# Attention's written order on TensorE: two scores ahead of each group's first transposes, and the first scores of a half spread out

## The chip, the cores and the metric

The kernel runs on one core of a Trainium2 chip. A core has five engines with a queue of instructions each: TensorE (PE, matrix products and transposes), VectorE (DVE), ScalarE (ACT), GpSimd (POOL) and SyncE (SP, which here issues transfers only). The metric is the time of one execution on the device in microseconds (us): the median of three runs of the kernel before is 2747.23 us (2744.07 to 2749.85).

## What is computed

One step of a one-layer encoder with two parallel mixers, on a prompt of 2048 rows and a sample of 64 rows with 4096 cached positions, width 1024. A combined projection gives q, k, v, gates and the input of a pooling branch. The attention branch has 8 heads of 128 and is "stick-breaking": no softmax, but a running product over the keys.

```python
    z = jnp.einsum('bqhd,bkhd->bhqk', q, k,
                   preferred_element_type=jnp.float32) * (SB_HEAD_DIM ** -0.5)
    mask = kpos[None, :] < qpos[:, None]
    log_beta = jax.nn.log_sigmoid(z)
    log_1m = jnp.where(mask, log_beta - z, 0.0)
    after = lax.cumsum(log_1m, axis=3, reverse=True) - log_1m
    a = jnp.where(mask, jnp.exp(log_beta + after), 0.0)
    out = jnp.einsum('bhqk,bkhd->bqhd', a, v.astype(jnp.float32))
```

So the weight of a key is sigmoid(z) times the product of 1 - sigmoid(z) over all later keys. The rest of the layer (pooling, gates, two output products, a merge, a residual and a norm) is not touched here.

## The kernel before

Every product is made in three matmuls, high by high, high by low and low by high part, from operands split by `split` (L77): a copy to the narrow form on ScalarE (L82) and a subtraction on VectorE or GpSimd (L83).

The prompt is done in two halves of 1024 rows. In a half, `heads_phase` (L842) goes over the heads: while head `hd + 1` is projected (`head_proj`, L482, through `proj`, L291), the attention of head `hd` runs between. `run` (L118) does the interleaving: each of its generators yields a step with its estimated length in ns, and `run` always takes the one that has had the smallest share of its total so far. A projection step is six matmuls. The estimates are written by hand: `mm_ns` (L107) for a matmul, `head_ns` (L619) for the attention of a head, `slab_ns` (L310) for the projections. `run` also adds the lengths to `clock`, by which deferred work (`defer`, L110, such as writing k and v out through transposes on PE, `natural`, L468) is started.

The attention of a half is a `Stream` (L605). Its units are tuples (head, block of 512 queries, chunk of 512 keys, i), newest chunk first, and four units with i = 0 to 3 make a group: one block of queries against one chunk of keys. A group whose chunk is the block itself is diagonal and is only partly computed. In the first half a head has 12 units, in the second 28. Three steps belong to a unit:

- `scores(n)`: three matmuls of 128 queries against the chunk (L641 to L643) into a bank `z`. Then `weights_of_block` (L580): two sigmoids on ScalarE (L585 `om`, L586 `be`), in diagonal groups two masks on GpSimd (L577), the carry of the chunk before copied by GpSimd (L590), a scan along the keys on VectorE (L595), the carry out (L597, GpSimd) and a multiply on VectorE (L598) that leaves the weights in `be`.
- `transposes(n)`: for 128 keys of the chunk, the weights of all the group's four query rows (in a diagonal group those from i on) are turned on PE (L654) and split into `a`, high and low. So the first `transposes` of a group needs `be` of all its four scores.
- `products(n)`: three matmuls of the values with `a` (L669 to L671); the third uses the low part.

`steps` (L680) sets the order: with n counting up, it yields `scores(n)`, `transposes(n - 4)`, `products(n - 5)`.

On PE the program's order is the order written (the whole kernel runs under a manual schedule for PE, L1519). In the heads' phases the order on the other engines is chosen by the scheduler of the framework, from readiness and program order. Tiles live in rings: eight `be`, three `om`, two `a`, and two banks each for `z`, `tr` and the projections' `pj`.

Of the kernel before, what the change touches and what calls it, by code (L numbers as in the profile page):

```python
# [15 lines left out]
P = 128  # L16
# [28 lines left out]
def kernel(  # L45
# [31 lines left out]
    def split(hi, lo, src, eng=None):  # L77

        if eng == "v":
            nc.vector.tensor_copy(hi, src)  # L80
        else:
            nc.scalar.copy(hi, src)  # L82
        (nc.gpsimd if eng == "g" else nc.vector).tensor_tensor(lo, src, hi.bitcast(F32), op=ALU.subtract)  # L83
# [23 lines left out]
    def mm_ns(n):  # L107
        return max(107.0, n * 0.4167)
# [37 lines left out]
    with ExitStack() as front:  # L146
# [433 lines left out]
        def weights_of_block(z, off, carry, diag=False, be=None):  # L580

            if be is None:
                be = attp.tile([P, 528], F32, name="be", tag="be", bufs=8)
            om = attp.tile([P, 513], F32, name="om", tag="om", bufs=3)
            nc.scalar.activation(om[:, off:512], z[:, off:512], AF.Sigmoid, scale=-SCALE)  # L585
            nc.scalar.activation(be[:, off:512], z[:, off:512], AF.Sigmoid, scale=SCALE)  # L586
            if carry is None:
                nc.gpsimd.memset(om[:, 512:513], 1.0)
            else:
                nc.gpsimd.tensor_copy(om[:, 512:513], carry)  # L590
            if diag:
                strictly_causal(om[:, 384:512], 1.0)
                strictly_causal(be[:, 384:512], 0.0)
            rev = om[:, off:513][:, ::-1]
            nc.vector.tensor_tensor_scan(rev, rev, rev, 1.0, op0=ALU.mult, op1=ALU.bypass)  # L595
            nxt = attp.tile([P, 1], F32, name="carry", tag="carry", bufs=10)
            nc.gpsimd.tensor_copy(nxt, om[:, off:off + 1])  # L597
            nc.vector.tensor_tensor(be[:, off:512], be[:, off:512], om[:, off + 1:513], op=ALU.mult)  # L598
            return be, nxt
# [5 lines left out]
        class Stream:  # L605
# [3 lines left out]
            def __init__(self, half):  # L609
                self.half = half  # L610
                self.units = [(hd, qb, c, i) for hd in range(H) for qb in (2 * half + 1, 2 * half)
                              for c in range(qb, -1, -1) for i in range(4)]
                self.n = 0
                self.be = {}
                self.carry = {}
                self.split = {}
                self.att = {}

            def head_ns(self, hd):  # L619
                return sum(3 * mm_ns(P * (i + 1)) + (4 - i) * 109 + 3 * mm_ns(P * (4 - i)) if c == qb else 1732.0  # L620
                           for h_, qb, c, i in self.units if h_ == hd)

            def scores(self, n):
                hd, qb, c, i = self.units[n]
                out = heads[self.half, hd]
                diag = c == qb
                for cc in range(2 * self.half - 1, -1, -1):
                    if cc in out["k"]:
                        continue
                    for kind, chunk in (("k", kchunk), ("v", vchunk)):  # L630
                        raw = attp.tile([P, 512], F32, name=f"{kind}back", tag=f"{kind}raw", bufs=2)
                        nc.sync.dma_start(raw, kvd[kind, hd, cc])
                        out[kind][cc] = chunk()
                        split(*out[kind][cc], raw, "g")
                khi, klo = out["k"][c]
                qhi, qlo = out["q"][qb]
                m = P * (i + 1) if diag else 512
                off = 512 - m
                z = psum.tile([P, 512], F32, name="z")
                qs = slice(i * P, (i + 1) * P)  # L640
                nc.tensor.matmul(z[:, off:512], qhi[:, qs], khi[:, 0:m], start=True, stop=False)  # L641
                nc.tensor.matmul(z[:, off:512], qhi[:, qs], klo[:, 0:m], start=False, stop=False)  # L642
                nc.tensor.matmul(z[:, off:512], qlo[:, qs], khi[:, 0:m], start=False, stop=True)  # L643
                be, self.carry[i] = weights_of_block(z, off, None if diag else self.carry[i], diag)
                self.be[hd, qb, c, i] = (be, off)
                return 3 * mm_ns(m)

            def transposes(self, n):
                hd, qb, c, j = self.units[n]
# [10 lines left out]
            def products(self, n):  # L660
# [16 lines left out]
                    nc.sync.dma_start(aT_d[hd * P:(hd + 1) * P, r0:r0 + 512], o)  # L677
                return 3 * mm_ns(512 - s.start)

            def steps(self, hd):  # L680

                end = len(self.units)
                while self.n < end + 5 and (hd is None or (self.n < end and self.units[self.n][0] == hd)):
                    n = self.n
                    self.n += 1
                    if n < end:
                        yield self.scores(n)
                    if 0 <= n - 4 < end:
                        yield self.transposes(n - 4)
                    if 0 <= n - 5 < end:  # L690
                        yield self.products(n - 5)


        def sample_stream():
# [135 lines left out]
            for n in range(-1, end + 2):  # L830
                if n + 1 < end:
                    yield from keys(n + 1)
                if 0 <= n < end:
                    yield scores(n)
                if 0 <= n - 1 < end:
                    yield transposes(n - 1)
                if 0 <= n - 2 < end:
                    yield products(n - 2)
# [338 lines left out]
    with tc.manual_schedule(engines={E.PE, E.DVE, E.Activation, E.SP}):  # L1177
# [4 lines left out]
        order = [(i, t, p) for i in range(2) for t in range(3) for p in range(7)]  # L1182
# [103 lines left out]
        for s, (i, t, p) in enumerate(order):  # L1286
            r = rf.pop(s)
            more = s - p + 7 < len(order)
            for cc in range(2):
# [5 lines left out]
                for j in range(2):  # L1295
                    c = 2 * cc + j
# [100 lines left out]
        for n, (_, r) in enumerate(pairs):  # L1397
            wo = {nm: wf.get((2, nm)) for nm in WFORMS}
            f = {nm: of.pop((n, nm)) for nm in ("a11", "a12", "s2", "s1")}
# [123 lines left out]
```

## Time and profile before

| What | Value |
|---|---|
| median of 3 runs | 2747.23 us |
| profiled execution, its own time | 2746.59 us |
| its span, first to last instruction | 2744.9 us |
| mean granted clock of PE | 0.994 |
| heads of the first half, about | 75 to 600 us |
| sample stream and the first half's gates, about | 600 to 1120 us |
| heads of the second half, about | 1160 to 1912 us |
| wait of the group's first transposes on `be`, as idle time | 3.4 us in 5 places |
| wait of the third product on the low part of `a`, as idle time | 3.4 us in 6 places |

A row of the timeline has a start in us from the start of the span, a length in us, the engine, the line, the operation, its tiles (out<-in) and shapes, and how many like it were merged. In brackets stands how long the engine had been idle before it, and what ended that. Matmuls overlap: a matmul's length includes its passage through the array, and the next starts before it ends. So idle time in brackets is shorter than the time that was lost, which is read from start to start.

### The profile page before, as it was taken

To read this page: it belongs to the slowest core of one execution; us is meant where nothing else is said; L and a number is where in the kernel's file an instruction comes from. 1 tells how busy PE (TensorE), PEld (TensorE's weight loads), DVE (VectorE), ACT (ScalarE), POOL (GpSimd) and SP (SyncE) were. 2 spreads that over 40 slices of the span, in tenths; PEclk is the share of its full clock that TensorE was granted. 3 is DMA by queue.
4 is the path that set the end of the run, shared out by engine and by line. 5 is a ranking of instruction groups with operands and counts; after the bars stand their busy time and mean duration, and the time that the engine had idled before them with its cause. 6 is when DMAs were issued, how large, how long until landed. Compare 5 with 4: busy or idle time off the path is not lost.

```text
span 2744.9 us, 41961 instructions
## 1 busy us (share of the span) xinstructions
PE 2700.3 (98%) x15136; PEld 2368.1 (86%) x15136; DVE 1831.3 (67%) x2866; ACT 1268.5 (46%) x2527; POOL 567.0 (21%) x1277
## 2 busy tenths in 40 slices
PE   8999999999999999999999999999999999999998
PEld 7988888888998989988888888888888889999886
DVE  5555555567777783487887888786454236777876
ACT  4445444455555553455555555564222223332443
POOL 1112222230000000222433333342004601111001
PEclk9999999999999999999999999999999999999999
DMA  4224222224444444312111211112236857786753
GB/s 133 87 89 128 73 73 73 77 94 153 151 155 152 148 146 145 100 35 66 48 38 54 58 47 50 54 43 85 94 104 215 270 179 269 258 289 223 250 162 119
DMA packets 343540, 342.32 MB, mean 125 GB/s; under 512 B 29969, under 2 KB 286465, under 8 KB 343330
## 3 DMA queue, kind: packets, MB, share of 16 engines
q1 hardware_dynamic: 328898, 292.69, 34.0%
q0 software_dynamic: 14432, 46.93, 4.8%
q8 instruction: 119, 1.95, 0.3%
q14 instruction: 91, 0.75, 0.1%
HBM read 230.90 MB, written 108.65 MB: 124 GB/s over the span
## 4 chain that ended last, share of the span: by engine, by line
PE 89%; DVE 5%; DMA 2%; issue 2%; ACT 1%; POOL 0%; SPq 0%; DVEq 0%; POOLq 0%; ACTq 0%
PE pj L299 17%; PE pj L300 17%; PE pj L301 17%; PE tr L654 4%; PE x L1083 3%; PE x L1085 3%; PE x L1087 3%; PE att L671 2%; PE att L670 2%; PE att L669 2%; PE z L643 2%; PE z L642 2%; PE z L641 2%; PE y L1083 2%; PE y L1085 2%; PE y L1087 2%
## 5 line engine op out<-in xcount | busy, mean ns | idle before, releaser
L299 PE MATMUL pj<-hhi,whi 128*128 128x512 f32 (+2 forms) x2568 | 929.7, 362 | 0.5 <-ACT hhi L886 0.5
L301 PE MATMUL pj<-hhi,wlo 128*128 128x512 f32 (+2 forms) x2568 | 902.7, 352 | 0.0
L300 PE MATMUL pj<-hlo,whi 128*128 128x512 f32 (+2 forms) x2568 | 901.9, 351 | 0.8 <-DVE hlo L889 0.7
L301 PEld LDWEIGHTS pj<-hhi,wlo 128*128 128x128 f32 x2568 | 487.3, 190 | 60.8
L299 PEld LDWEIGHTS pj<-hhi,whi 128*128 128x128 f32 x2568 | 489.5, 191 | 56.6 <-ACT hhi L886 1.2
L300 PEld LDWEIGHTS pj<-hlo,whi 128*128 128x128 f32 x2568 | 488.7, 190 | 56.0 <-DVE hlo L889 1.5
L595 DVE TENSOR_TENSOR_SCAN om<-om 128x513 f32<-128x513 f32 (+3 forms) x356 | 387.5, 1088 | 209.8 <-POOL om L577 108.1
L585 ACT ACTIVATE om<-z 128x512 f32<-128x512 f32 (+2 forms) x320 | 171.6, 536 | 320.1 <-PE z L643 270.5
L83 DVE TENSOR_TENSOR wlo<-raw,whi 128x512 fp32r<-128x512 f32 x244 | 174.4, 719 | 184.8 <-ACT whi L82 183.9
L597 POOL COPY carry<-om 128x1 f32<-128x1 f32 x356 | 78.6, 221 | 915.0 <-DVE om L595 871.5
L598 DVE TENSOR_TENSOR be<-be,om 128x512 f32<-128x512 f32 (+3 forms) x356 | 230.5, 647 | 33.3 <-ACT a L82 0.5
L82 ACT CAST whi<-raw 128x512 fp32r<-128x512 f32 x251 | 155.1, 623 | 173.3 <-PE pj L300 160.2
L82 ACT CAST a<-tr 128x512 fp32r<-128x512 f32 (+2 forms) x356 | 188.0, 528 | 100.2 <-PE tr L654 89.8
L83 DVE TENSOR_TENSOR a<-tr,a 128x512 fp32r<-128x512 f32 (+2 forms) x356 | 215.6, 606 | 25.0 <-ACT a L82 23.1
L654 PE MATMUL tr<-ident,be 128*128 128x128 f32 x1088 | 176.1, 274 | 6.0 <-DVE be L598 3.4
L654 PEld LDWEIGHTS tr<-ident,be 128*128 128x128 f32 x1088 | 136.2, 140 | 44.4 <-DVE be L598 8.5
L586 ACT ACTIVATE be<-z 128x512 f32<-128x512 f32 (+2 forms) x320 | 170.0, 531 | 0.0
L669 PE MATMUL att<-a,v 128*128 128x512 f32 (+1 forms) x320 | 132.6, 414 | 0.0
L577 POOL TENSOR_SCALAR_AFFINE_SELECT om<-om 128x128 f32<-128x128 f32 x128 | 50.6, 395 | 359.6 <-ACT om L585 345.9
L590 POOL COPY om<-carry 128x1 f32<-128x1 f32 x224 | 123.4, 551 | 2.7 <-DVE be L598 0.7
L671 PE MATMUL att<-a,v 128*128 128x512 f32 (+1 forms) x320 | 118.6, 371 | 3.7 <-DVE a L83 3.4
L643 PE MATMUL z<-khi,qlo 128*128 128x512 f32 (+2 forms) x320 | 116.8, 365 | 0.0
(333 smaller groups left out, 4758.1 us busy)
## 6 DMA issues: line engine op xcount, KB each, us to landing
raw<-in_w_in_dram SPq DMA_DIRECT2D x253, 256.0 KB, 3.0
sg<-sm_d SPq DMA_DIRECT2D x48, 352.0 KB, 6.5
kraw<-in_cache_k_dram SPq DMA_DIRECT2D x64, 256.0 KB, 3.2
vraw<-in_cache_v_dram SPq DMA_DIRECT2D x64, 256.0 KB, 2.9
sm_d<-sgm SPq DMA_DIRECT2D x48, 256.0 KB, 2.4
wraw<-tw_d SPq DMA_DIRECT2D x24, 512.0 KB, 4.2
out_dram<-nat SPq DMA_DIRECT2D x42, 256.0 KB, 3.3
r<-aT_d SPq DMA_DIRECT2D x12, 704.0 KB, 7.3
```

What stands on the lines that cost most here:

```text
L82: nc.scalar.copy(hi, src)
L83: (nc.gpsimd if eng == "g" else nc.vector).tensor_tensor(lo, src, hi.bitcast(F32), op=ALU.subtract)
L299: nc.tensor.matmul(ps[:, 0:n], whi[:, k], hhi[:, k, c0:c0 + n], start=k == 0, stop=False)
L300: nc.tensor.matmul(ps[:, 0:n], whi[:, k], hlo[:, k, c0:c0 + n], start=False, stop=False)
L301: nc.tensor.matmul(ps[:, 0:n], wlo[:, k], hhi[:, k, c0:c0 + n], start=False, stop=k == KT - 1)
L585: nc.scalar.activation(om[:, off:512], z[:, off:512], AF.Sigmoid, scale=-SCALE)
L595: nc.vector.tensor_tensor_scan(rev, rev, rev, 1.0, op0=ALU.mult, op1=ALU.bypass)
L598: nc.vector.tensor_tensor(be[:, off:512], be[:, off:512], om[:, off + 1:513], op=ALU.mult)
L643: nc.tensor.matmul(z[:, off:512], qlo[:, qs], khi[:, 0:m], start=False, stop=True)
L654: nc.tensor.transpose(tr[:, i * P:(i + 1) * P], be[:, off + j * P:off + (j + 1) * P], ident)
L669: nc.tensor.matmul(self.acc[:, s], vhi[:, js], ahi[:, s], start=first, stop=False)
L671: nc.tensor.matmul(self.acc[:, s], vhi[:, js], alo[:, s], start=False, stop=last)
```

## The change

`steps` no longer counts units but takes its steps from a list that the new `order` makes. For each group with first unit g it gives: scores g and g + 1, transposes g - 4, products g - 5; then scores g + 2, transposes g - 3, products g - 4; then scores g + 3, transposes g - 2, products g - 3; then transposes g - 1, products g - 2. Before, one score stood ahead of each transposes. The second part is `lead`: the first four scores of a half count 1500 ns more each in `run`, and so does their head in `head_ns`. The steps themselves are as they were.

```diff
-                self.att = {}
+                self.todo = list(self.order())
 
             def head_ns(self, hd):
-                return sum(3 * mm_ns(P * (i + 1)) + (4 - i) * 109 + 3 * mm_ns(P * (4 - i)) if c == qb else 1732.0
-                           for h_, qb, c, i in self.units if h_ == hd)
+                return sum((3 * mm_ns(P * (i + 1)) + (4 - i) * 109 + 3 * mm_ns(P * (4 - i)) if c == qb else 1732.0)
+                           + self.lead(n) for n, (h_, qb, c, i) in enumerate(self.units) if h_ == hd)
+
+            def lead(self, n):
+                return 1500.0 if n < 4 else 0.0
...
-                return 3 * mm_ns(m)
+                return 3 * mm_ns(m) + self.lead(n)
...
+            def order(self):
+                end = len(self.units)
+                for g in range(0, end + 4, 4):
+                    for i in range(4):
+                        for n in ((g, g + 1), (g + 2,), (g + 3,), ())[i]:
+                            if n < end:
+                                yield n, self.scores, n
+                        for f, n in ((self.transposes, g + i - 4), (self.products, g + i - 5)):
+                            if 0 <= n < end:
+                                yield g, f, n
+                yield end, self.products, end - 1
+
             def steps(self, hd):
 
-                end = len(self.units)
-                while self.n < end + 5 and (hd is None or (self.n < end and self.units[self.n][0] == hd)):
-                    n = self.n
-                    self.n += 1
-                    if n < end:
-                        yield self.scores(n)
-                    if 0 <= n - 4 < end:
-                        yield self.transposes(n - 4)
-                    if 0 <= n - 5 < end:
-                        yield self.products(n - 5)
+                while self.todo and (hd is None or (self.todo[0][0] < len(self.units)
+                                                    and self.units[self.todo[0][0]][0] == hd)):
+                    _, f, n = self.todo.pop(0)
+                    yield f(n)
```

## The prediction, made before the changed kernel was run

> **What bounds the kernel.** I read the busy table first, then the table by stretches, then the waits of TensorE (PE), then the timeline of single groups.
>
> ```profile
> PE 2700.3 (98%) x15136; PEld 2368.1 (86%) x15136; DVE 1831.3 (67%) x2866; ACT 1268.5 (46%) x2527; POOL 567.0 (21%) x1277
> PEclk9999999999999999999999999999999999999999
> 1160.00:1820.00 660.00, 653.98 (x3333) 538.18 (x3333) 537.69 (x733) 381.25 (x773) 227.16 (x550) 1.00 0.17 50
> PE tr L654 <- DVE be L598: 3.4, 5, 1.9
> PE att L671 <- DVE a L83: 3.4, 6, 0.6
> ```
>
> PE is busy in 98% of the span at full clock, in an order written out by hand. So an edit of that order can only take away, or add, moments in which PE stands still: nothing is computed more or less. The third row is the attention of the second half (columns: length, PE, weight loads, VectorE (DVE), ScalarE, GpSimd): PE is busy for 654.0 of 660 us and VectorE for 537.7, 81%. VectorE makes everything that attention waits for there. The two wait rows count only idle time behind modelled ends; I therefore take lost time from the starts in the timeline.
>
> Names: **S** is a unit's score step (three matmuls), **T** its transposes, **P** its three products, **J** a step of six projection matmuls. Four units, 0 to 3, make a group. T needs the weights `be` of all four scores of its group; P's third matmul (L671) needs the low part `a` that VectorE subtracts after its T.
>
> **What the change removes.** The wait of a group's first T for the fourth score's `be`. Before, one S stands between that score's own step and T; now there are two, and a T and a P more.
>
> ```profile
> 1358.70 0.83 PE L654 MATMUL tr<-ident,be 128*128 128x128 f32 x4
> 1359.29 0.48 PE L299 MATMUL pj<-hhi,whi 128*128 128x512 f32 x1
> 1428.46 0.60 PE L654 MATMUL tr<-ident,be 128*128 128x128 f32 x4
> 1428.82 0.48 PE L669 MATMUL att<-a,v 128*128 128x512 f32 x1
> 1429.13 0.40 PE L670 MATMUL att<-a,v 128*128 128x512 f32 x1
> 1430.09 0.50 PE L671 MATMUL att<-a,v 128*128 128x512 f32 x1 [0.56 <-DVE a L83]
> 1162.11 0.34 PE L643 MATMUL z<-khi,qlo 128*128 128x384 f32 x1
> 1162.67 0.50 PE L641 MATMUL z<-khi,qhi 128*128 128x512 f32 x1 [0.23 <-ACT be L586]
> 1165.56 0.85 PE L654 MATMUL tr<-ident,be 128*128 128x128 f32 x3
> 1168.36 0.33 PE L654 MATMUL tr<-ident,be 128*128 128x128 f32 x1 [1.94 <-DVE be L598]
> 1168.44 0.48 PE L299 MATMUL pj<-hhi,whi 128*128 128x512 f32 x1
> 1901.51 0.85 PE L654 MATMUL tr<-ident,be 128*128 128x128 f32 x4
> 1902.12 0.48 PE L299 MATMUL pj<-hhi,whi 128*128 128x512 f32 x1
> ```
>
> An undisturbed T of four takes 0.36 from its start to the next matmul (1428.46 to 1428.82). The one at 1358.70 takes 0.59, the last at 1901.51 takes 0.61, and the half's first at 1165.56 takes 2.88. From 578 to 1902 us there are 23 such places, together 7.0 us; the half's first is 2.5 of it. The 1500 ns of `lead` put J steps between the first four scores of a half; with them the fourth score's wait for a `z` bank goes too (1162.11 to 1162.67, 0.5 with its second matmul). The J steps that come early are missing later, so they cost nothing. I take all **7.5** as gone. The bound on the other side is that the half's start stays: 3.0 less.
>
> There are also waits of L671. At 1429.13 the third product starts 0.96 after the second where 0.23 is usual, so 0.73 is lost. This place comes six times (heads 1 to 6), 4.4 in all; in the new order one more J stands between that T and its P, 1.4 us, so I count it as gone (bound: it stays). Nine smaller ones add 1.8. Removed in all: 7.5 + 4.4 + 1.8 = **13.7**.
>
> **What it moves.** The last quarter of a group now has no score. T2 P1 T3 P2 follow the fourth score, and P2 comes one S earlier behind its T2 than before. I stepped through the picking rule of `run` with its own estimates (43,868 of attention against 40,963 of projection per head in the second half). For head 2, units counted in the half, the order was J S78 T74 P73 J S79 T75 P74 S80; it becomes S79 J T74 P73 T75 P74 S80. The old stretch as it ran, PE, then ScalarE, then VectorE:
>
> ```profile
> 1419.94 0.38 PE L654 MATMUL tr<-ident,be 128*128 128x128 f32 x2
> 1420.69 0.39 PE L299 MATMUL pj<-hhi,whi 128*128 128x512 f32 x1
> 1422.07 0.39 PE L641 MATMUL z<-khi,qhi 128*128 128x512 f32 x1
> 1422.75 0.27 PE L654 MATMUL tr<-ident,be 128*128 128x128 f32 x1
> 1422.78 0.36 PE L669 MATMUL att<-a,v 128*128 128x256 f32 x1
> 1422.98 0.28 PE L670 MATMUL att<-a,v 128*128 128x256 f32 x1
> 1423.31 0.38 PE L671 MATMUL att<-a,v 128*128 128x256 f32 x1
> 1423.54 0.40 PE L641 MATMUL z<-khi,qhi 128*128 128x512 f32 x1
> 1420.20 0.60 ACT L585 ACTIVATE om<-z 128x512 f32<-128x512 f32 x1 [1.64 <-PE z L643]
> 1421.17 0.38 ACT L82 CAST a<-tr 128x256 fp32r<-128x256 f32 x1
> 1420.90 1.23 DVE L595 TENSOR_TENSOR_SCAN om<-om 128x513 f32<-128x513 f32 x1 [0.61 <-ACT om L585]
> 1422.23 0.69 DVE L598 TENSOR_TENSOR be<-be,om 128x512 f32<-128x512 f32 x1
> 1422.84 0.42 DVE L83 TENSOR_TENSOR a<-tr,a 128x256 fp32r<-128x256 f32 x1
> ```
>
> A score ends on PE at 1419.94. Its scan and its multiply run on VectorE ahead of the subtraction of the T that follows, and that subtraction ends at 1423.26, 3.32 after the score. On PE, T74 and P73 take 0.75 (1419.94 to 1420.69), J 1.38 (to 1422.07), S79 0.68 (to 1422.75), T75 and two products 0.35 (L670 would be followed after 0.12, at 1423.10). So L671 is reached 3.16 after the score and waits 0.21 until 1423.31. Without S79 in between it is reached 0.75 + 1.38 + 0.35 = 2.48 after the score, and the same 3.32 + 0.05 makes it wait **0.89**. What is queued behind it on PE is everything: the next two scores, and so the next scans. Where J stands, ahead of T74 or behind P73, makes no difference to this sum.
>
> The terms of what is added:
>
> - P2 of the diagonal groups, 16 in the second half, one J each between the fourth score and P2: 16 x 0.89 = **14.2**. Bounds: 0.18 each if VectorE takes the subtraction ahead of the multiply (first rival), and 1.4 us more where the next item bites.
> - Eight of them stand at the start of a head, seven behind another head, where GpSimd is held up:
>
> ```profile
> 1362.13 0.39 PE L299 MATMUL pj<-hhi,whi 128*128 128x512 f32 x1
> 1362.35 1.31 POOL L83 TENSOR_TENSOR v<-vback,v 128x512 fp32r<-128x512 f32 x1 [1.28 <-ACT v L82]
> 1363.59 1.12 POOL L590 COPY om<-carry 128x1 f32<-128x1 f32 x1
> 1364.67 1.29 POOL L675 TENSOR_TENSOR ao<-ao,sga 128x512 f32<-128x512 f32 x1
> 1364.84 1.68 DVE L598 TENSOR_TENSOR be<-be,om 128x512 f32<-128x512 f32 x1
> ```
>
>   The scan must wait for GpSimd's copy of the carry (1.12 behind the split of `vback`), and the multiply takes 1.68 for 0.69. A score ends on PE at 1362.13, where the first row's projection follows it, and its multiply at 1366.52: 4.4, where the undisturbed one above takes 2.98. In the new order the score after it is the one that counts, so I take not quite half of the 1.4: 7 x 0.6 = **4.2**. Bounds: 0 and 9.8.
> - P2 of the full groups with no J between score and T2, 23 of them: reached after 1.13 (T2 and P1) + 1.38 + 0.90 (T3, two products; from the rows at 1428.46) = 3.41; needed after 3.32, or 3.58 with the larger subtraction. 0 to 0.22 each; I take the middle, 23 x 0.1 = **2.3**. With a J between they have 1.4 to spare: nothing.
> - The tail of the first half, where projections run thin: two such P2, 0.9 + 0.5 = **1.4**. Elsewhere in that half two J steps and more stand between: nothing.
> - Two double scores with no spare time, in the first group of the half and in the tail: 0.5 + 0.6 = **1.1** (bounds 0 and 3).
>
> Nothing else moves: of the memory rings (eight `be`, three `om`, two `a`, banks in twos) none is taken earlier than its last reader stands in PE's order; the loads of old keys and values still go out with a head's first score. Ahead of a group's last T stands the same set of steps as before, so the six waits behind the doubled `natural` stay. The two scores in front bunch four VectorE operations, 3.5 us, ahead of P0 and P1, but these keep 3.3 to 5.0 us behind their T against some 3.1: covered. If that cover went, each would cost a few tenths.
>
> The sum: 14.2 + 4.2 + 2.3 + 1.4 + 1.1 = 23.2 added, 13.7 removed, **+9.5 us**. The profiled execution took 2746.59 (span 2744.9 and 1.69 around it), 0.64 under the median 2747.23; so 2756.1 against it, 2756.7 against the median.
>
> The Trainium skill ("TensorE: Matmul & The Clock Gate", "Back-to-back issue gap") gives about 131 ns per matmul of 512 columns in a sustained stream. By that J would take 0.79, P2 would come 0.59 earlier, and the sum would rise by 16 x 0.59 = 9.4 to about 2766. Here six take 1.38, 230 ns each, and I go by that.
>
> **The rivals.** *VectorE takes the subtraction first.* Its order is not written by hand but chosen by the scheduler. For it:
>
> ```profile
> 1423.71 1.23 DVE L595 TENSOR_TENSOR_SCAN om<-om 128x513 f32<-128x513 f32 x1 [0.45 <-ACT om L585]
> 1424.85 0.26 DVE L83 TENSOR_TENSOR a<-tr,a 128x128 fp32r<-128x128 f32 x1
> 1425.04 0.69 DVE L598 TENSOR_TENSOR be<-be,om 128x512 f32<-128x512 f32 x1
> ```
>
> Here it stands between scan and multiply. Then each diagonal P2 waits 0.71 less (1422.84 against 1422.13, the scan's end), 0.18. With 16 x 0.71 = 11.4 and the 2.3 off, 9.5 added against 13.7 removed: -4.2, and -8.4 if the head starts do not bite either; about 2740. It decides from the 14th site on (9.5 / 0.71 = 13.4). Against it: this case is a narrow T of 128 columns; for those of 256, the order is scan, multiply, subtraction in all but two of the 31 in the trace that follow a score.
>
> *Gain and loss cancel.* Head starts (4.2) and full groups (2.3) cost nothing: +3.0, 2750. For it: before, the head starts show no wait of L671. Against: there P had 0.7 us more.
>
> *GpSimd's splits fall into the new bunches.* The head starts cost 1.2 each (+4.2) and the six 0.73 waits go along (+4.4): 2765. The Trainium skill ("SBUF — State Buffer", "SBUF: two separate sides") says that VectorE with two inputs in SBUF and GpSimd exclude one another for a whole instruction; the multiply of 1.68 above, which ended 0.56 after GpSimd's product, bears that out.
>
> *The spreading doesn't work*, and the half's first T still waits: +3.0, 2760.
>
> **How the numbers follow.** Forecast 0.37; GpSimd's splits 0.10 and no spreading 0.06 (all slower); cancelling 0.27; subtraction first 0.20. Under 0.2%, 5.5 us, this kernel can't be told from no change. Slower 0.53, same 0.27, faster 0.20. Range 2738 (both parts of the first rival) to 2768; the forecast's own is 2752 to 2763.
>
> **What would show it.** First transposes: no wait for `be` over 0.1 us, and none at the second half's start. L671's waits for `a`: about 20 us by starts, near 0.9 at each diagonal P2, and hardly any at P0, P1, P3. PE's six projection matmuls still 1.38. I am wrong if the multiply runs behind the subtraction at the diagonal P2, if waits turn up at P0 or P1, or if P2 isn't where they are.

## The result, and the profile after

The changed kernel takes **2771.39 us** (median of 4 runs, 2769.72 to 2774.78), the kernel before in the same series 2745.98 us (2744.07 to 2749.85): a ratio of **1.0093, 95% interval 1.0079 to 1.0107**. It is slower by about 25 us, where 9.5 were forecast, and 3 us above the range. The span of the profiled execution went from 2744.9 to 2773.1 us, +28.2. Ratios and intervals here and below are estimated from the single runs, so they can differ in the fourth place from the quotient of two medians, and one slow run of e2 (7691 us) counts in no ratio.

In the changed kernel the scores are L644 to L646, the transposes L657, the products L672 to L674. The busy table and the clock, from the page of the changed kernel:

```profile
PE 2708.4 (98%) x15136; PEld 2368.1 (85%) x15136; DVE 1827.7 (66%) x2866; ACT 1269.2 (46%) x2527; POOL 561.7 (20%) x1277
PEclk9999999999999999999999999999999999999999
```

PE does the same number of matmuls at the same clock. The table by stretches, same stretch of the second half as before (columns: length, then busy time of PE, weight loads, VectorE, ScalarE, GpSimd):

```profile
1160.00:1820.00 660.00, 639.59 (x3231) 521.71 (x3230) 521.33 (x707) 372.38 (x747) 218.74 (x531) 1.00 0.17 49
```

PE gets through 3231 matmuls in the 660 us, where it was 3333, and is busy for 639.6 instead of 654.0. All engines get through some 3% fewer instructions: the whole stretch runs later. The table of PE's waits (total idle time, places, longest) says behind what:

```profile
PE att L674 <- DVE a L83: 20.6, 33, 1.8
PE tr L657 <- ACT nat L476: 3.5, 8, 1.3
PE tr L657 <- DVE a L83: 3.1, 6, 0.5
```

The row of the first transposes that waited for `be` has gone (3.4 in 5 places before). The third product's wait for the low part of `a` went from 3.4 in 6 places to 20.6 in 33, and transposes now wait for `a` too, through a bank of `tr`.

Idle time is only part of it. From start to start, beside what the same pair of matmuls usually takes, the second half loses 24.9 us more than before: the third products 27.8 in 44 places (6.2 in 15 before), the transposes on a bank 4.0 in 6 places (none before). The first half loses 2.6 more. It is regular: heads 1 to 6 of the second half (counted from 0) take 97.2 us each where they took 93.95.

**The place that the prediction stepped through**, one head later. PE, then VectorE, then GpSimd in the timeline of the changed kernel:

```profile
1526.28 0.40 PE L646 MATMUL z<-khi,qlo 128*128 128x512 f32 x1
1526.51 0.39 PE L299 MATMUL pj<-hhi,whi 128*128 128x512 f32 x1
1527.91 0.38 PE L657 MATMUL tr<-ident,be 128*128 128x128 f32 x2
1528.81 0.27 PE L657 MATMUL tr<-ident,be 128*128 128x128 f32 x1
1529.04 0.28 PE L673 MATMUL att<-a,v 128*128 128x256 f32 x1
1530.79 0.39 PE L674 MATMUL att<-a,v 128*128 128x256 f32 x1 [1.47 <-DVE a L83]
1531.02 0.39 PE L644 MATMUL z<-khi,qhi 128*128 128x512 f32 x1
```
```profile
1523.89 1.58 DVE L598 TENSOR_TENSOR be<-be,om 128x512 f32<-128x512 f32 x1
1525.40 0.68 DVE L83 TENSOR_TENSOR wlo<-raw,whi 128x512 fp32r<-128x512 f32 x1
1526.00 1.21 DVE L595 TENSOR_TENSOR_SCAN om<-om 128x513 f32<-128x513 f32 x1
...
1528.39 1.22 DVE L595 TENSOR_TENSOR_SCAN om<-om 128x513 f32<-128x513 f32 x1
1529.71 0.69 DVE L598 TENSOR_TENSOR be<-be,om 128x512 f32<-128x512 f32 x1
1530.32 0.62 DVE L83 TENSOR_TENSOR a<-tr,a 128x256 fp32r<-128x256 f32 x2
```
```profile
1523.64 1.29 POOL L678 TENSOR_TENSOR ao<-ao,sga 128x512 f32<-128x512 f32 x1
1524.87 0.65 POOL L590 COPY om<-carry 128x1 f32<-128x1 f32 x1
```

The order is the forecast one: the fourth score, J, T2 and P1, T3, P2. The score ends at 1526.51. The third product of P2 is reached at 1529.16 (0.12 behind the second) and starts at 1530.79, **1.63 late**, where 0.89 was forecast. Scan, multiply and subtraction follow one another as forecast; but VectorE comes to this score's scan only at 1528.39. It is still at the score before: GpSimd's gate product holds the multiply up from 1523.89 (1.58 for 0.69) and stands ahead of the copy of the carry; then come a subtraction of the projections and a late scan. Subtraction done: 1530.74, 4.2 after the score instead of 3.32.

**A full group.** Here the four scores in front are the diagonal ones of the next head. PE, VectorE, GpSimd:

```profile
1553.20 0.60 PE L657 MATMUL tr<-ident,be 128*128 128x128 f32 x4
1556.38 0.40 PE L673 MATMUL att<-a,v 128*128 128x512 f32 x1
1557.14 0.50 PE L674 MATMUL att<-a,v 128*128 128x512 f32 x1 [0.37 <-DVE a L83]
```
```profile
1554.45 1.23 DVE L595 TENSOR_TENSOR_SCAN om<-om 128x513 f32<-128x513 f32 x1 [1.07 <-POOL om L577]
1555.79 0.69 DVE L598 TENSOR_TENSOR be<-be,om 128x512 f32<-128x512 f32 x1
1556.40 0.68 DVE L83 TENSOR_TENSOR a<-tr,a 128x512 fp32r<-128x512 f32 x1
```

The score ends at 1553.20. Its scan is released by GpSimd's mask, which was not in the forecast, and starts 1.25 after the score, where the undisturbed one of the prediction started after 0.96. The subtraction ends 3.9 after the score, and the third product is 0.53 late. This comes seven times. Ahead of another full group the third product loses 0.22, the upper end that the prediction gave, in one full group of each of heads 1 to 7. In heads 1 to 6 a third thing happens, in the first full group; PE, then VectorE:

```profile
1486.12 0.60 PE L474 MATMUL tr<-ident,kst 128*128 128x128 f32 x4
...
1487.02 0.40 PE L674 MATMUL att<-a,v 128*128 128x512 f32 x1
1487.93 0.66 PE L657 MATMUL tr<-ident,be 128*128 128x128 f32 x4 [0.51 <-DVE a L83]
```
```profile
1487.19 0.68 DVE L83 TENSOR_TENSOR a<-tr,a 128x512 fp32r<-128x512 f32 x1
```

The transposes that write out projected keys or values (`natural`, L474) take one of the two `tr` banks between T2 and T3. So T3 needs the bank of T2, and that is free only when the same late subtraction has read it: 0.67 lost, and P2 behind it finds its `a` ready. The wait that P2 would have had stands one step earlier.

**The start of a head.** P1, not only P2, waits there, behind a scan of 2.09 for the usual 1.22, which overlaps GpSimd's gate product (1468.74 to 1470.03); PE, then VectorE:

```profile
1471.57 0.33 PE L673 MATMUL att<-a,v 128*128 128x384 f32 x1
1472.43 0.45 PE L674 MATMUL att<-a,v 128*128 128x384 f32 x1 [0.54 <-DVE a L83]
```
```profile
1469.02 2.09 DVE L595 TENSOR_TENSOR_SCAN om<-om 128x513 f32<-128x513 f32 x1 [0.79 <-ACT om L585]
1471.22 0.69 DVE L598 TENSOR_TENSOR be<-be,om 128x512 f32<-128x512 f32 x1
1471.83 0.55 DVE L83 TENSOR_TENSOR a<-tr,a 128x384 fp32r<-128x384 f32 x1
```

Two more places, at the halves' starts: the first T of the second half no longer waits (0.36 to the next matmul, 1173.26 to 1173.62), but in the first half a T now waits for ScalarE's copy out of `tr`, 1.5 us, and 1.1 at 1181 in the second:

```profile
118.97 0.49 PE L474 MATMUL tr<-ident,kst 128*128 128x128 f32 x3
120.72 0.41 PE L657 MATMUL tr<-ident,be 128*128 128x128 f32 x2 [1.25 <-ACT nat L476]
...
1173.26 0.60 PE L657 MATMUL tr<-ident,be 128*128 128x128 f32 x4
1173.62 0.48 PE L299 MATMUL pj<-hhi,whi 128*128 128x512 f32 x1
```

### The profile page after: what moved, and what is told of

Its sections match the earlier page's. It is cut to its first block, busy times and chain, and to the rows that moved or that the text cites. A ratio compares the mean times of both kernels' runs of the same rounds, so it can differ in the third digit from the quotient of the medians.

```text
span 2773.1 us, 42048 instructions
## 1 busy us (share of the span) xinstructions
PE 2708.4 (98%) x15136; PEld 2368.1 (85%) x15136; DVE 1827.7 (66%) x2866; ACT 1269.2 (46%) x2527; POOL 561.7 (20%) x1277
## 5 line engine op out<-in xcount | busy, mean ns | idle before, releaser
L597 POOL COPY carry<-om 128x1 f32<-128x1 f32 x356 | 70.4, 198 | 964.3 <-DVE om L595 923.4
L657 PE MATMUL tr<-ident,be 128*128 128x128 f32 x1088 | 171.4, 273 | 6.5 <-ACT nat L476 3.5
L657 PEld LDWEIGHTS tr<-ident,be 128*128 128x128 f32 x1088 | 135.6, 140 | 38.8 <-DVE a L83 5.7
L674 PE MATMUL att<-a,v 128*128 128x512 f32 (+1 forms) x320 | 122.5, 383 | 21.3 <-DVE a L83 20.6
L672 PE MATMUL att<-a,v 128*128 128x512 f32 (+1 forms) x320 | 130.2, 407 | 0.4 <-ACT a L82 0.4
L646 PE MATMUL z<-khi,qlo 128*128 128x512 f32 (+2 forms) x320 | 116.9, 365 | 0.0
```

The lines of the kernel that those rows point to most:

```text
L657: nc.tensor.transpose(tr[:, i * P:(i + 1) * P], be[:, off + j * P:off + (j + 1) * P], ident)
L672: nc.tensor.matmul(self.acc[:, s], vhi[:, js], ahi[:, s], start=first, stop=False)
```

## The experiments

The theory: products stand too near behind their own transposes, because a score's scan and multiply run ahead of the subtraction that they need. The rivals: the spreading (`lead`) costs the time; GpSimd's work does, wherever the products stand. Third product means the third matmul of a P step; P2 is the P step of unit 2 of a group.

| Kernel | median, us | to the kernel before, 95% interval |
|---|---|---|
| the change | 2771.39 | 1.0093 [1.0079, 1.0107] |
| e1: new order, no spreading | 2770.17 | 1.0087 [1.0070, 1.0103] |
| e2: old order, spreading | 2744.57 | 0.9993 [0.9983, 1.0003] |
| e3: multiply written behind the subtraction | 2771.92 | 1.0089 [1.0074, 1.0104] |
| e4: P2 two scores later | 2741.60 | 0.9980 [0.9971, 0.9990] |
| e5: no gate product | 2762.60 | 1.0060 [1.0045, 1.0075] |
| e6: e3, and VectorE kept to it | 2742.80 | 0.9991 [0.9982, 1.0000] |
| e7: e4 without spreading | 2742.65 | 0.9987 [0.9977, 0.9996] |
| e8: e4, spreading not in the head's clock | 2743.57 | 0.9985 [0.9974, 0.9996] |
| e9: old order with e6's multiply, no spreading | 2745.55 | 1.0003 [0.9993, 1.0013] |
| e10: e4 and e6 together | **2732.37** | **0.9954 [0.9940, 0.9969]** |
| e11: old order where a diagonal group is transposed | 2756.45 | 1.0043 [1.0028, 1.0058] |

The experiments were timed in three series, each beside the kernel before (2747.37, 2746.5 and 2744.9 us). Where two of them are compared below, the difference of their ratios is taken and multiplied by 2746 us.

**The two parts apart: e1 and e2.** In e1 `lead` gives nothing; e2 has `lead` and the old `steps`.

```diff
             def lead(self, n):
-                return 1500.0 if n < 4 else 0.0
+                return 0.0
```

> The changed kernel without the spreading (lead is 0). If the new order is what costs, the time stays near 2771 us: the half's first T keeps part of its wait (some 1 us instead of 2.5, as two scores stand ahead of it now), and the waits of T on the banks of tr behind the transposes of k and v (1.5 us at 120.7, 1.1 at 1181.6 in the changed kernel) go. If the spreading is what costs beyond the forecast, it is 2762 or less.

> The spreading alone, with the old order. By the prediction the wait at the start of the second half (3.0 us) goes and nothing is paid: 2743. If the spreading pays for itself with the early transposes of k and v (its clock runs 6 us ahead), 2746, no change.

The order alone costs as much as the whole change. The spreading alone makes no difference that can be measured; the 3.0 us that it was to save would be 0.11%, and the interval of e2 reaches from -0.17% to +0.03%. PE's waits in e1:

```profile
PE att L674 <- DVE a L83: 23.4, 34, 1.8
...
PE tr L657 <- DVE a L83: 3.4, 6, 0.8
```

The waits are those of the change. So the rest is about the order.

**VectorE's order: e3 and e6.** The multiply of `be` is no longer issued with its score, but by the next transposes, behind their subtraction; e6 also pins it to that place. Both edits, shortened:

```diff
+            def weigh():
+                return nc.vector.tensor_tensor(be[:, off:512], be[:, off:512], om[:, off + 1:513], op=ALU.mult)
+            if late is None: weigh()
+            else: late.append(weigh)
...
+                while self.late:               # in transposes, behind the split
+                    self.late.pop(0)()         # e3
+                    tc.keep_in_program_order(self.late.pop(0)())   # e6, in place of e3's line
```

> The changed kernel with the multiply that finishes be written behind the split of the next transposes, so that VectorE takes the subtraction first. If the multiply ahead of the subtraction is what makes each P2 late, some 32 places get 0.6 us back: 2771 - 15 = 2756 (at most 0.69 x 32 = 22). If the lateness lies in the scans before it, the subtraction still ends late: 2766 or more.

> The changed kernel with the multiply written behind the subtraction of the next transposes, and pinned there, so that VectorE really takes the subtraction first (writing it later without the pin had left VectorE's order as it was). If the multiply's place is what makes P2 late, every wait of P2 gets up to 0.69 us shorter and most vanish: some 32 places, 2771 - 18 = 2753. If the scans are late already, the waits only shrink a little: 2765 or more. A loss can come from be being ready later: the first transposes would wait again.

e3 changes neither the time nor VectorE's order. VectorE in e3 at the place shown above:

```profile
1526.20 1.22 DVE L595 TENSOR_TENSOR_SCAN om<-om 128x513 f32<-128x513 f32 x1
1527.52 0.69 DVE L599 TENSOR_TENSOR be<-be,om 128x512 f32<-128x512 f32 x1
1528.13 0.61 DVE L83 TENSOR_TENSOR a<-tr,a 128x256 fp32r<-128x256 f32 x2
```

The multiply (now L599) still stands ahead of the subtraction, though it is written behind it: the scheduler put it there all the same. So e3 says nothing about the multiply's place. e6 is the same program with the place kept. PE, then VectorE in e6:

```profile
1512.76 0.28 PE L684 MATMUL att<-a,v 128*128 128x256 f32 x1
1513.48 0.39 PE L685 MATMUL att<-a,v 128*128 128x256 f32 x1 [0.44 <-DVE a L83]
```
```profile
1511.89 1.22 DVE L595 TENSOR_TENSOR_SCAN om<-om 128x513 f32<-128x513 f32 x1
1513.03 0.40 DVE L83 TENSOR_TENSOR a<-tr,a 128x256 fp32r<-128x256 f32 x1
1513.34 0.68 DVE L599 TENSOR_TENSOR be<-be,om 128x512 f32<-128x512 f32 x1
```

Now the subtraction stands between scan and multiply, and the third product is 0.60 late (0.72 behind the second for 0.12) instead of 1.63. The kernel's time falls by 1.02%, 28 us: everything that the change had cost, and more than the 18 expected; T3's six waits on the bank go as well (4.0 us by starts), which the expectation had not counted. With PE's order unchanged, the place of the multiplies on VectorE takes the loss away, so it is shown to be a cause; the two scores in front cost nothing by themselves. Some waits are left: by starts the third products of the second half still lose 8.4 us, where the change lost 27.7.

**The distance on PE: e4.** P2 of each group is put behind the next group's first two scores, so that the subtraction has time whatever VectorE's order is (shortened):

```diff
-                    for i in range(4):
-                        for n in ((g, g + 1), (g + 2,), (g + 3,), ())[i]: ...
+                    for f, n in ((self.scores, g), (self.scores, g + 1), (self.products, g - 6),
+                                 (self.transposes, g - 4), (self.products, g - 5),
+                                 (self.scores, g + 2), (self.transposes, g - 3), (self.products, g - 4),
+                                 (self.scores, g + 3), (self.transposes, g - 2), (self.products, g - 3),
+                                 (self.transposes, g - 1)): ...
```

> The changed kernel with one step moved: the third products of a group stand behind the two scores of the next group instead of directly behind the last transposes. If the nearness of P2 to its T2 is the whole cost, its waits for a go (about 20 of the 23.7 us by starts) and with them the waits of T for a (4.0): about 2747, as before or a little under. If the bunched scores make VectorE late whatever stands where, the waits come back at P0, P1 or P3: over 2758.

PE's waits in e4:

```profile
PE tr L657 <- ACT nat L476: 4.7, 8, 1.3
...
PE tr L657 <- DVE a L83: 3.1, 6, 0.5
...
PE att L674 <- DVE a L83: 2.2, 4, 0.9
```

The products' waits fall from 20.6 to 2.2, the time by 1.13%, 31 us, and the kernel is a little faster than before the change. T3's six waits on the bank stay, as they must: T3 did not move. Either cure, e4's on PE or e6's on VectorE, makes up for the whole loss. So the loss at P2 needs two things at once, the nearness of P2 to its T2 and the multiply ahead of the subtraction. The two cures are not the same, though: e4 leaves T3's waits, e6 leaves part of P2's, and e10 below has neither.

**GpSimd's part: e5.** GpSimd's product of the attention with its gate is left out.

```diff
-                    nc.gpsimd.tensor_tensor(o, o, heads[self.half, hd]["g"][qb][:, 0:512], op=ALU.mult)
```

> The changed kernel without the gate's product on GpSimd that follows the last product of a block of queries (the output leaves out that gate). If GpSimd's long operations ahead of the carry copies make the scans late, the diagonal P2 in mid-head waits about 0.9 us as forecast instead of 1.63, with the like at the tails: 2771 - 7 = 2764. If the two scores in front make VectorE late by themselves, its wait stays over 1.4 and the time within 2 us of 2771.

The time falls by 0.33%, 9 us. PE in e5 at the same kind of place:

```profile
1523.70 0.28 PE L673 MATMUL att<-a,v 128*128 128x256 f32 x1
1524.62 0.39 PE L674 MATMUL att<-a,v 128*128 128x256 f32 x1 [0.64 <-DVE a L83]
```

0.92 between the two products, so 0.80 late, near the 0.89 that the prediction had worked out without the gate product. At the start of the same head the scan is back to its usual length:

```profile
1464.44 1.23 DVE L595 TENSOR_TENSOR_SCAN om<-om 128x513 f32<-128x513 f32 x1 [0.78 <-ACT om L585]
```

P1's wait there has gone, and P2's is about 0.5. By starts, the third products of the second half lose 18.1 us instead of 27.7: 5.4 of the difference lie at the diagonal groups in the middle of a head, 4.0 at the head starts. The other two thirds of the kernel's loss stay. So GpSimd's gate product makes the waits longer, and alone makes the one of P1; it does not make the rest.

**Which groups: e11.** Where the group whose products are made is a diagonal one, one score stands ahead of each transposes again.

```diff
+                    diag = 4 <= g < end + 4 and self.units[g - 4][1] == self.units[g - 4][2]
-                        for n in ((g, g + 1), (g + 2,), (g + 3,), ())[i]:
+                        for n in ((g + i,) if diag else ((g, g + 1), (g + 2,), (g + 3,), ())[i]):
```

> The changed kernel with the old interleaving wherever a diagonal group's products are made, so the two scores in front stand only where a full group's products are made. By the prediction the diagonal places carry 18.4 of the 20.7 us at the P2 of the second half: 2771 - 18 = 2753. By the trace of the changed kernel they carry about 2.7 us a head of 4.2, so 19 of 27: 2752, and the full groups' 1.4 a head stay. If VectorE is late by the two scores as such, wherever they stand, 2760 or more.

14 us go (0.50%) and 0.43%, 12 us, stay. Not all of the 12 are the full groups' of the changed kernel. By starts, 6.4 us of e11 stand at P0 and P1 of the full group behind a diagonal one, where the change loses 0.5 and the kernel before lost 4.4: a wait of e11's own order. But the full groups' waits of the change are all still there: 0.22 and 0.53 at P2, 0.67 at T3's bank. PE's waits in e11:

```profile
PE att L674 <- DVE a L83: 7.0, 20, 1.0
PE tr L657 <- DVE a L83: 3.9, 7, 0.8
```

**The waits for `nat`: e7 and e8.** In e4 they are 4.7 us, 1.2 more than in the change. e7 is e4 with `lead` giving nothing, e8 is e4 with one line more in `scores`, so that the spreading doesn't move the clock that the head's other steps are timed by.

```diff
+                clock[0] -= self.lead(n)
```

> Two scores in front, the third products behind the next two scores, and no spreading. Against the same kernel with the spreading (2741.6) it tells what the spreading does there: if its early transposes of k and v cost as much as it saves, no difference, 2741 to 2743; if the spreading saves its 3 us, 2744 to 2745; if it costs, 2739.

> Two scores in front, the third products behind the next two scores, and the spreading without its effect on the clock of the deferred work. If the clock is what brings the transposes of k and v forward into waits for banks (1.5 us in the first half, 1.1 and 0.9 in the second), this kernel is 2 to 3 us under the one with the full spreading: 2739. If not, 2741.6.

The three times can't be told apart. In e7 these waits fall to `2.4, 6, 0.4`, in e8 they stay at 4.7, so the clock is not behind them; the spread order itself is. That it gives back elsewhere what it costs there fits the times, but is not shown.

**Whether the cure needs the change: e9 and e10.** e9 is the kernel before with e6's pinned multiply; e10 is e4 with it.

> The old order, without spreading, with the multiply pinned behind the subtraction of the next transposes. The waits of the third product (6.2 us) go, but be is ready later where a single score stands ahead of the first transposes: those waits grow by up to 0.7 us at some 40 groups of the second half. If the multiply's place matters only together with the room that the new order makes, 2755 to 2770; if subtraction first is simply better, 2740.

> Two scores in front, the third products behind the next two scores, and the multiply pinned behind the subtraction. If both edits cure the same waits (of the third product for the low part of a), they do not add up: 2738 to 2742. If each cures another part, 2735 or less. A loss is possible where be gets late: 2745.

In the old order the pinned multiply changes nothing that can be measured. The waits of the third product have gone, but those of the first transposes have grown from 3.4 us to 8.5; PE's waits in e9:

```profile
PE tr L660 <- DVE be L599: 8.5, 8, 1.9
```

A later multiply is a later `be`, and the old order has only one score of room for it. With two scores in front there is room: e6 and e10 show no wait of the transposes for `be`. e10 is the fastest kernel of the study, 0.46% under the kernel before [0.31%, 0.60%]. It is 0.26%, 7 us, under e4 and 0.37%, 10 us, under e6, so by what was expected of it each cure takes away a part that the other leaves. No third product and no T waits for `a` in its table, and the first row there is

```profile
PE tr L663 <- ACT nat L476: 4.5, 8, 1.3
```

## Why the prediction was right and wrong

Right were the direction, the mechanism and the first place where it bites: P2 comes too early behind its T2, since scan and multiply stand ahead of the subtraction. e6 and e4 show it from both sides. Right was also what is removed: no first transposes wait for `be` any more, and the six 0.73 waits have gone. PE's six projection matmuls still take 1.40 (1526.51 to 1527.91). The rule of the Trainium skill that the prediction weighed ("TensorE: Matmul & The Clock Gate", "Back-to-back issue gap", about 131 ns for 512 columns) would make it 0.79 by estimate. The trace does not agree, here as before.

The size was wrong, by its terms. Second half, lost time from start to start:

| Term | forecast, us | measured, us |
|---|---|---|
| first T's waits for `be`, and the `z` bank | -7.5 | -6.3 |
| old waits of the third product | -6.2 | -6.2 |
| diagonal groups, head starts included | +18.4 | +19.4: six of 1.63, one of 1.93, seven starts of 1.1 |
| full groups | +2.3 | +10.0: 6.0 at P2, 4.0 at T3's bank |
| other places (first head, tail, double scores) | +1.1 | +2.4 |
| matmuls behind a stop, 0.1 late each | 0 | +3.3 |
| waits for `nat`, two single transposes | 0 | +2.1 |
| sum | +8.1 | +24.7 |

The first half took 2.6 more, for 1.4. Together that is 27.3 of the 28.2; the last 0.9 is not traced. Of the 16.6 us that the second half lost beyond the forecast, the full groups make 7.7, the matmuls behind a stop 3.3 and the waits for `nat` and single transposes 2.1.

- **The step that failed** is the lateness of VectorE, "needed after 3.32, or 3.58 with the larger subtraction", and with it "23 x 0.1 = 2.3" for the full groups. Both figures came from an undisturbed stretch. In the changed kernel the subtraction comes 4.2 after the score in the middle of a head, behind GpSimd's gate product, where 3.32 was taken; and it comes 3.9 after where the scores in front are the next head's diagonal ones and GpSimd's mask releases the scan, where 3.58 was taken. Full groups lost 10.0, twice the upper bound of 23 x 0.22 = 5.1: 6.0 at P2 in 16 places, 4.0 at T3's bank in six.
- In the diagonal groups the sum came out right by luck, from two errors: 1.63 for 0.89 in the middle of a head, 1.1 for 0.89 + 0.6 at its start.
- "None is taken earlier than its last reader stands in PE's order" was wrong for the `tr` banks. Where the transposes of `natural` stand between T2 and T3, the late subtraction holds up T3 and not P2: six times 0.67.
- "P0 and P1 ... covered" held but for P1 at the head starts, 0.7 of the 1.1 there. Waits at P1 were one of the prediction's own signs of being wrong.
- Nothing was counted for the start of PE behind each stop. A matmul there is followed 0.1 later than usual (1530.79 to 1531.02 is 0.23, where 0.12 is usual behind 256 columns); over some 30 stops more than before that is 3.3 us.
- That `lead` costs nothing fits: e1, e2 and e7 show no difference from it. For the same reason the 3.0 us that it was to save are seen in the trace (the half's first T no longer waits) but not in the time.

Of the rivals, "VectorE takes the subtraction first" didn't happen by itself, since the scheduler puts the multiply first. Forced to it in e6, the kernel came out at 2742.8, and the rival's forecast was about 2740. Its price was near, though not place by place: P2 is still 0.60 late in the middle of a head, where the rival had 0.18. Its condition was not met. "GpSimd's splits fall into the new bunches" came nearest in time (2765) and named the right engine. But its terms did not come: the head starts lost 1.1 each, less than the 1.5 of the forecast and the 2.1 of this rival, and the six waits of 0.73 went. What e5 shows is the gate product, 9 us, at the head starts and in the middle of a head; the splits alone were not tested. "Gain and loss cancel" and "the spreading doesn't work" fell: the losses bite in 50 places, and the second half's first T no longer waits.

## What to carry to other kernels

When an operation is moved nearer to what it waits for, take the lateness of that input from the most disturbed stretch that will come to stand there, not from a clean one, and follow every reader of the same late instruction: the one whose bank it frees as well as the one that uses its result. Where a loss hangs on the order of two ready instructions on a scheduled engine, writing them in another order may move nothing; pinning the order did (28 us in the changed order, 7 in e4's). In the old order the same pin moved nothing that can be measured (e9): much of what it saved at the third products came back at the first transposes.

## What was unexpected of the hardware

VectorE's multiply took 1.58 us instead of 0.69 where it started 0.25 behind GpSimd's gate product (1523.89 and 1523.64); it ended 0.54 after the product's end at 1524.93, about as if it had begun only then. The rule that the prediction cited from the Trainium skill ("SBUF — State Buffer", "SBUF: two separate sides") is that of VectorE with two inputs in SBUF and a GpSimd instruction that reads SBUF, the one that starts first holds the other up for its whole instruction; the trace agrees with that. The scan at a head's start behaves alike: 2.09 us beside the gate product, 1.23 in e5 without it. What follows from it was not expected: 0.9 us on VectorE in the middle of a head comes out as 0.83 us (1.63 against 0.80 in e5) on PE, whose wait there is for VectorE and not for GpSimd.
